# Turning u of two MLPs: from TensorE transposes to transposing DMAs on 16-bit halves

## The chip, the cores and the metric

The kernel runs on one core of one Trainium2 chip. A core has five engines that run their own instruction streams side by side: TensorE (PE in the profile, with its weight loads as PEld), VectorE (DVE), ScalarE (ACT), GpSimd (POOL) and SyncE (SP). All transfers of this kernel are issued from SP's queue, in order, and sixteen DMA engines carry them out. The metric is the device time of one execution in microseconds. The kernel before takes 2280.91 us in the median of three runs (2279.25 to 2284.33).

## The reference

The reference is a decoder trunk of two layers on 256 tokens of width 2048, in float32. Layer 0 has a convolution module as its token mixer, layer 1 differential attention, and each layer ends with the same kind of MLP. Every sub-layer scales and shifts its input by values made from a condition vector c (`mod = silu(c) @ ada_w + ada_b`), and ends in a LayerNorm. The part that the change touches is the MLP, which is computed twice:

```
def squared_relu_mlp(h, w1, b1, w2, b2):
    u = jnp.square(jax.nn.relu(h @ w1 + b1))
    return u @ w2 + b2
```

Here h is 256 x 2048, w1 is 2048 x 8192 and w2 is 8192 x 2048.

## The kernel before

**Arithmetic.** Each float32 operand of a large product is split into a high part (rounded to the float32r type) and a low part (the rest). A product is made of three matmuls: high by high, high by low, low by high (L700, L702, L703). The weights are split on the way: a 1 MB tile of 128 x 2048 comes from memory into one of four `raw` buffers, and each of its two halves is cast by ACT into `wh` (L655, "cast" below) and subtracted by DVE into `wl` (L657). There are four buffers each for `wh` and `wl` (`N_SP = 4`), so the cast of a half can run when PE has left the half four places before it.

**Tiling of an MLP.** The 8192 hidden columns are worked off in four quarters (q = 0 to 3). A quarter has four groups of w1 (g = 0 to 3), each making 512 columns of u for both token tiles (t = 0, 1), and then four groups of w2, which add that quarter's share of the output. A group has 4 weight tiles, so 8 halves, and a half feeds 12 matmuls of 128 x 512. In the two MLPs together there are 32 groups of w1, 16 each.

**Turning u.** A group of w1 leaves `h @ w1` in PSUM with tokens on the partitions, and w2 needs it with hidden columns on the partitions. `on_t1` is called when a token tile of a group is complete: ACT copies the PSUM tile to SBUF (`us`, L1452); two ticks later (`U_WAIT = 2`, a tick is one half) PE turns it by four 128 x 128 transposes into another PSUM tile (`ut`, L1458). Bias, relu and square follow: in the first MLP relu with bias on ACT in four pieces (L1464) and the square on ACT for q = 0 (L1467) and on DVE for the rest (L1469); in the second MLP an addition (L1471) and a max-multiply (L1474) on DVE. At last ACT casts the result to `u_hi` (L513) and DVE subtracts to `u_lo` (L516). All this is `on_t1` with its inner `rest`, and `put_split`. u's parts are read by w2's matmuls; the four groups of u are used one after the other, 4 of 16 chunks each.

**What else runs then.** During the first MLP, and the first quarter of the second, rows of `ada_w` come in as 1 MB tiles (`adaw`) through the same four `raw` buffers, and DVE takes their dot product with the condition (L228, one instruction of 2048 columns per tile). Small transfers bring rows for the residual (`basem_gb`, `basem_b`).

**What sets the order.** The kernel is written as a list of jobs whose steps are recorded in program order, with `defer(n, f)` putting a step n ticks later. A scheduler of the framework then sorts every engine's instructions by its own estimate of time. On the chip each engine works off its stream strictly in that order: an instruction whose operand is late holds all that stand behind it on its engine. The same holds for SP: a transfer that waits for a buffer or a source holds the transfers behind it.

Of the kernel before, what the change touches and what calls it, by code (L numbers as in the profile page):

```python
# [11 lines left out]
F32 = mybir.dt.float32  # L12
F32R = mybir.dt.float32r
I32 = mybir.dt.int32
AF = mybir.ActivationFunctionType
ALU = mybir.AluOpType
AX = mybir.AxisListType
# [2 lines left out]
P = 128  # L20
# [5 lines left out]
NG = 512  # L26
# [21 lines left out]
AHEAD = 4  # L48
POOL_LO = ()
U_WAIT = 2  # L50
POOL_LEAD = ()
POOL_TAIL = ()
GF_LOAD = 16
# [102 lines left out]
def trunk(  # L156
# [8 lines left out]
    nc = tc.nc  # L165
# [5 lines left out]
    work = ctx.enter_context(tc.tile_pool(name="work", bufs=2))  # L171
# [69 lines left out]
    def defer(n, fn):  # L241
        put_off.append((ticks[0] + n, fn))
# [265 lines left out]
    def put_split(pair, c0, n, s0, ns, src, eng=None, trail=False):  # L508

        hi, lo = pair  # L510
        h = hi[:, c0:c0 + n, s0:s0 + ns]
        l = lo[:, c0:c0 + n, s0:s0 + ns]
        nc.scalar.copy(h, src)  # L513

        def low():
            (eng or nc.vector).tensor_tensor(l, src, h.bitcast(F32), op=ALU.subtract)  # L516
        if trail:
            trailing.append(low)
        else:
            low()  # L520
# [464 lines left out]
    for g in range(NGRP):  # L985
# [3 lines left out]
    cv = {}  # L989

    cv.update(pw1b=vec1[:, 96:128], dwb=vec1[:, 128:144], clng=vec1[:, 144:160], clnb=vec1[:, 160:176],
              b1c=vec1[:, 176:304], lnc=vec1[:, 304:432], subg=vec1[:, 432:434])
# [267 lines left out]
    for s, (f0, nf) in enumerate(SLICES):  # L1260
# [6 lines left out]
        for pos, k in units:  # L1267
            g = group_order(s)[pos]
# [136 lines left out]
    for q in range(4):  # L1405
        defer(4 + q, lambda q=q: alpha_x(q))

    def mlp(i, ln_g, ln_b, gcol, bcol, pump, at_end, start=None, mid=None, last=None):
        gate, sc, cur = {}, {}, {}
        st = stats_tile(f"mlp{i}")  # L1410
# [35 lines left out]
        for q in range(4):  # L1446
            for g in range(4):
                n0 = q * D + g * NG

                def on_t1(t, ps, q=q, g=g, n0=n0):  # L1450
                    us = work.tile([P, NG], F32, tag="A", name=f"us_{i}_{q}_{g}_{t}")
                    nc.scalar.copy(us, ps)  # L1452
                    uT = cur["uT"]

                    def rest():
                        pt = tp_tile(f"ut_{i}_{q}_{g}_{t}")
                        for j in range(4):
                            nc.tensor.transpose(out=pt[:, j * P:(j + 1) * P], in_=us[:, j * P:(j + 1) * P],  # L1458
                                                identity=ident)
                        r = work.tile([P, 4, P], F32, tag="B", name=f"r_{i}_{q}_{g}_{t}")  # L1460
                        f0 = i * 64 + n0 // P
                        if i == 0:
                            for j in range(4):
                                nc.scalar.activation(r[:, j, :], pt[:, j * P:(j + 1) * P], AF.Relu,  # L1464
                                                     bias=cv["b1c"][:, f0 + j:f0 + j + 1])
                            if q == 0:
                                nc.scalar.activation(r, r, AF.Square)  # L1467
                            else:
                                nc.vector.tensor_tensor(r, r, r, op=ALU.mult)  # L1469
                        else:  # L1470
                            nc.vector.tensor_tensor(r, pt.rearrange("p (a n) -> p a n", a=4),  # L1471
                                                    cv["b1c"][:, f0:f0 + 4].unsqueeze(2).broadcast_to([P, 4, P]),
                                                    op=ALU.add)
                            nc.vector.scalar_tensor_tensor(r, r, 0.0, r, ALU.max, ALU.mult)  # L1474
                        put_split(uT, g * 4, 4, t * P, P, r, trail=True)
                    defer(U_WAIT, rest)
                first = q == 0 and g == 0
                add_group(f"w1_{i}_{q}_{g}", lambda: cur["hT"], wtiles(mlp_w1[i], 0, KC, n0), pump=pump, lead=(i + 1) * first,
                          start=(lambda q=q: begin_q(q)) if g == 0 else None,
                          pre_t=pre_t if first else None, on_t=on_t1, prep=(i == 1, prep) if first else None,  # L1480
                          between=ada_between if first and i == 0 else None)
            for n in range(4):
                def on_t2(t, ps, q=q, n=n):
                    add_gated(ps, gate["gb"], t, n, f"w2g_{i}_{q}_{n}_{t}")
                    if q == 3:
                        nc.vector.bn_stats(st[t][:, n, :], z[:, t, n * NG:(n + 1) * NG])
                        if n == 3:
                            return at_end(st, t)
                        if last is not None and t == 1 and n in (1, 2):
                            last["product"](t, n)  # L1490
                add_group(f"w2_{i}_{q}_{n}", lambda: cur["uT"], wtiles(mlp_w2[i], q * KC, KC, n * NG), pump=pump,
                          start=(lambda q=q: begin_w2(q)) if n == 0 else None,
                          tail=(q == 3 and n == 3) * (2 if last is None else 3), on_t=on_t2)
# [385 lines left out]
```

## Time and profile before

| | |
|---|---|
| median of 3 runs | 2280.91 us (2279.25 to 2284.33) |
| the profiled execution's own time | 2280.64 us |
| its span, first to last instruction | 2278.9 us |
| busy in the span | PE 2244.4 us, DVE 1714.8 us, ACT 1082.1 us, POOL 38.3 us |
| granted TensorE clock | 0.996 |
| moved by DMA | 608.58 MB, 267 GB/s in the mean |
| first MLP, about | 416 to 1146 us of the span |
| second MLP, about | 1546 to 2240 us of the span |

Times in the profile are counted from the first instruction. A row of the groups' view gives line, engine, operation, output and inputs, shape, how often, then busy microseconds, the mean nanoseconds of one, and the engine's idle time just before such instructions with what ended it. A row of the timeline starts with start and duration in microseconds. The windows' view gives for each stretch the busy time of each engine and how many instructions, then the granted clock, the mean busy share of the sixteen DMA engines and the rate.

### The profile page before, as it was taken

Reading aid. Unit: us, or ns where it says so; the run is one execution under the profiler, and the core shown is the slowest. Engines: PE = TensorE matmul, PEld = TensorE weight load, DVE = VectorE, ACT = ScalarE, POOL = GpSimd, SP = SyncE. Lnnn points to the kernel's source line nnn. Section 1 sums busy time; section 2 is a strip of 40 time slices with the busy share of each in tenths; the row PEclk is TensorE's granted clock in tenths of the full one; section 3 lists DMA queues with packets and bytes.
Section 4 is the critical chain, followed back from the end, with each engine's and each line's share of the span. In section 5 each row is a group of like instructions: output and inputs, shape, how many; then the busy total and the mean of one; then the engine's idle time right before and its main releaser. Section 6 shows DMA issues by size and latency. Waiting matters only on the chain.

```text
span 2278.9 us, 28170 instructions
## 1 busy us (share of the span) xinstructions
PE 2244.4 (98%) x11060; PEld 1797.1 (79%) x11060; DVE 1714.8 (75%) x2124; ACT 1082.1 (47%) x1488; POOL 38.3 (2%) x53
## 2 busy tenths in 40 slices
PE   8999999999999999999999999999999999999999
PEld 5677657687888888888878888877888888888886
DVE  7687989787978888777878877877866565655656
ACT  4336763564355355355454445545444444443442
POOL 0000000000000000000000010100000000000000
PEclk9999999999999999999999999999999999999999
DMA  9996789699988988988757766775965555556563
GB/s 397 420 394 257 312 324 396 215 338 323 347 302 305 320 288 309 325 290 311 279 176 248 241 222 208 279 269 172 331 233 188 186 194 193 185 185 203 185 222 111
DMA packets 217473, 608.58 MB, mean 267 GB/s; under 512 B 10382, under 2 KB 10610, under 8 KB 187770
## 3 DMA queue, kind: packets, MB, share of 16 engines
q1 hardware_dynamic: 217340, 606.78, 74.6%
q8 instruction: 87, 1.43, 0.3%
q14 instruction: 46, 0.38, 0.0%
HBM read 604.59 MB, written 2.15 MB: 266 GB/s over the span
## 4 chain that ended last, share of the span: by engine, by line
PE 87%; DVE 6%; ACT 3%; DMA 3%; issue 1%; POOL 0%; SPq 0%; ACTq 0%; DVEq 0%; POOLq 0%
PE w_ps L700 20%; PE w_ps L702 20%; PE w_ps L703 20%; PE pw_ps L598 2%; PE pw_ps L599 2%; PE pw_ps L600 2%; PE cv L934 1%; PE pw_ps L700 1%; PE pw_ps L703 1%; PE ut L1458 1%; PE qkv_v_ps L703 1%; PE pw_ps L702 1%; PE qkv_v_ps L700 1%; PE qkv_v_ps L702 1%; PE qkv_q_ps L703 1%; PE qkv_q_ps L700 1%
## 5 line engine op out<-in xcount | busy, mean ns | idle before, releaser
L655 ACT CAST wh_w<-w_w 128x1024 fp32r<-128x1024 f32 x512 | 536.2, 1054 | 692.1 <-PE w_ps L703 524.4
L657 DVE TENSOR_TENSOR wl_w<-w_w,wh_w 128x1024 fp32r<-128x1024 f32 x510 | 614.4, 1221 | 330.5 <-ACT wh_w L655 330.3
L700 PE MATMUL w_ps<-wh_w,hm_hi 128*128 128x512 f32 x1024 | 402.3, 393 | 2.4 <-ACT hm_hi L513 2.4
L702 PE MATMUL w_ps<-wl_w,u_hi 128*128 128x512 f32 x1024 | 399.1, 390 | 2.3 <-DVE wl_w L657 2.3
L703 PE MATMUL w_ps<-wh_w,hm_lo 128*128 128x512 f32 x1024 | 399.5, 390 | 1.6 <-DVE hm_lo L516 1.6
L700 PE MATMUL w_ps<-wh_w,u_hi 128*128 128x512 f32 x1024 | 399.5, 390 | 0.0
L702 PE MATMUL w_ps<-wl_w,hm_hi 128*128 128x512 f32 x1024 | 399.5, 390 | 0.0
L703 PE MATMUL w_ps<-wh_w,u_lo 128*128 128x512 f32 x1024 | 398.6, 389 | 0.0
L228 DVE SCALAR_TENSOR_TENSOR adaw<-adaw,cond_rows 128x2048 f32<-128x2048 f32 x108 | 246.6, 2284 | 0.1
L700 PEld LDWEIGHTS w_ps<-wh_w,hm_hi 128*128 128x128 f32 x1024 | 192.7, 188 | 44.6 <-ACT hm_hi L513 3.9
L703 PEld LDWEIGHTS w_ps<-wh_w,hm_lo 128*128 128x128 f32 x1024 | 192.7, 188 | 43.2 <-DVE hm_lo L516 2.9
L702 PEld LDWEIGHTS w_ps<-wl_w,u_hi 128*128 128x128 f32 x1024 | 192.2, 188 | 43.6 <-DVE wl_w L657 4.4
L700 PEld LDWEIGHTS w_ps<-wh_w,u_hi 128*128 128x128 f32 x1024 | 192.2, 188 | 40.3
L703 PEld LDWEIGHTS w_ps<-wh_w,u_lo 128*128 128x128 f32 x1024 | 192.2, 188 | 40.1
L702 PEld LDWEIGHTS w_ps<-wl_w,hm_hi 128*128 128x128 f32 x1024 | 192.8, 188 | 39.0
L598 PE MATMUL pw_ps<-wh_pw,h_hi 128*128 128x512 f32 x256 | 103.8, 405 | 2.2 <-ACT wh_pw L580 1.5
L599 PE MATMUL pw_ps<-wl_pw,h_hi 128*128 128x512 f32 x256 | 100.8, 394 | 0.9 <-DVE wl_pw L583 0.8
L600 PE MATMUL pw_ps<-wh_pw,h_lo 128*128 128x512 f32 x256 | 100.6, 393 | 0.0
L583 DVE TENSOR_TENSOR wl_pw<-w_pw,wh_pw 128x1024 fp32r<-128x1024 f32 x64 | 77.2, 1219 | 28.9 <-ACT wh_pw L580 28.6
L580 ACT CAST wh_pw<-w_pw 128x1024 fp32r<-128x1024 f32 x64 | 65.9, 1051 | 44.6 <-PE pw_ps L600 27.9
L598 PEld LDWEIGHTS pw_ps<-wh_pw,h_hi 128*128 128x128 f32 x256 | 48.4, 189 | 29.3 <-issue 12.6
L516 DVE TENSOR_TENSOR u_lo<-r,u_hi 128x512 fp32r<-128x512 f32 x64 | 43.5, 688 | 19.1 <-ACT u_hi L513 17.9
(350 smaller groups left out, 2991.2 us busy)
## 6 DMA issues: line engine op xcount, KB each, us to landing
w_w<-in_mlp_w_dram SPq DMA_DIRECT2D x256, 1024.0 KB, 5.5
adaw<-in_ada_rows_dram SPq DMA_DIRECT2D x108, 1024.0 KB, 6.9
w_pw<-in_pw_tiles_dram SPq DMA_DIRECT2D x32, 1024.0 KB, 11.6
ad<-in_ada_rows_dram SPq DMA_DIRECT2D x25, 1024.0 KB, 8.8
w_pw<-in_conv_pw_w_dram SPq DMA_DIRECT2D x16, 1024.0 KB, 9.7
w_qkv_q<-in_attn_qkv_w_dram SPq DMA_DIRECT2D x16, 1024.0 KB, 5.1
w_qkv_k<-in_attn_qkv_w_dram SPq DMA_DIRECT2D x16, 1024.0 KB, 5.0
w_qkv_v<-in_attn_qkv_w_dram SPq DMA_DIRECT2D x16, 1024.0 KB, 6.7
```

The costliest lines, as they stand in the source:

```text
L228: nc.vector.scalar_tensor_tensor(w, w, 1.0, cond_rows, ALU.mult, ALU.mult, accum_out=m[:, ch:ch + 1])
L516: (eng or nc.vector).tensor_tensor(l, src, h.bitcast(F32), op=ALU.subtract)
L580: nc.scalar.copy(hq, rq)
L583: nc.vector.tensor_tensor(lq, rq, hq.bitcast(F32), op=ALU.subtract)
L598: nc.tensor.matmul(pss[t], lhsT=xh, rhs=wh, start=(kc == first), stop=False)
L599: nc.tensor.matmul(pss[t], lhsT=xh, rhs=wl, start=False, stop=False)
L600: nc.tensor.matmul(pss[t], lhsT=xl, rhs=wh, start=False, stop=(kc == last))
L655: nc.scalar.copy(hi, rq)
L657: eng.tensor_tensor(lo, rq, hi.bitcast(F32), op=ALU.subtract)
L700: nc.tensor.matmul(pss[tt], lhsT=xh, rhs=wh, start=(kc == 0 and job["bias"] is None), stop=False)
L702: nc.tensor.matmul(pss[tt], lhsT=xh, rhs=wl, start=False, stop=False)
L703: nc.tensor.matmul(pss[tt], lhsT=xl, rhs=wh, start=False, stop=(kc == nk - 1))
```

## The change

In both MLPs (`BY_DMA = (0, 1)`) u is now turned by DMA in place of PE. The DMA turns 16-bit elements, so each float32 is handled as two of them. `on_t1` hands over to a new function `halves_t`, which, for each token tile of a group, does the following:

- ACT copies the PSUM tile to SBUF as before (now L1419), save for g = 1, t = 1 (`DIRECT`), where this copy is left out and the next step reads PSUM.
- ACT copies the tile once more (L1421), as 1024 elements of 16 bits, so that the 512 first halves stand together and then the 512 second halves.
- SP issues a transposing DMA within SBUF (L1423), 128 x 1024 elements of 16 bits in eight blocks of 128 x 128.
- Four ticks later in the program (`T_WAIT = 4`), ACT joins the halves again into float32 (L1427), and bias, relu, square and split follow, from SBUF and not from PSUM. In the first MLP's q = 0 the square moves from ACT to DVE.

There are 64 token tiles in the two MLPs, 8 of them direct.

```diff
+T_WAIT = 4
+BY_DMA = (0, 1)
+DIRECT = ((1, 1),)
...
+    def halves_t(t, ps, uT, i, q, g, n0):
+
+        name = f"{i}_{q}_{g}_{t}"
+        room = work.tile([P, 2, NG], F32, tag="X", name=f"us_{name}", bufs=3)
+        us = ps
+        if (g, t) not in DIRECT:
+            us = room[:, 0, :]
+            nc.scalar.copy(us, ps)
+        parts = room[:, 1, :].bitcast(U16).rearrange("p (b n) -> p b n", b=2)
+        nc.scalar.copy(parts, us.bitcast(U16).rearrange("p (n b) -> p b n", b=2))
+        turned = work.tile([P, 2, 4, P], U16, tag="A", name=f"ux_{name}")
+        nc.sync.dma_start_transpose(turned.rearrange("p b a n -> p (b a) n"), parts.rearrange("p b n -> p (b n)"))
+
+        def rest():
+            r = work.tile([P, 4, P], F32, tag="B", name=f"r_{name}")
+            nc.scalar.copy(r.rearrange("p a n -> p (a n)").bitcast(U16).rearrange("p (a n b) -> p a n b", a=4, b=2),
+                           turned.rearrange("p b a n -> p a n b"))
+            f0 = i * 64 + n0 // P
+            if i == 0:
+                for j in range(4):
+                    nc.scalar.activation(r[:, j, :], r[:, j, :], AF.Relu, bias=cv["b1c"][:, f0 + j:f0 + j + 1])
+                nc.vector.tensor_tensor(r, r, r, op=ALU.mult)
+            else:
+                nc.vector.tensor_tensor(r, r, cv["b1c"][:, f0:f0 + 4].unsqueeze(2).broadcast_to([P, 4, P]), op=ALU.add)
+                nc.vector.scalar_tensor_tensor(r, r, 0.0, r, ALU.max, ALU.mult)
+            put_split(uT, g * 4, 4, t * P, P, r, trail=True)
+        defer(T_WAIT, rest)
...
                 def on_t1(t, ps, q=q, g=g, n0=n0):
+                    uT = cur["uT"]
+                    if i in BY_DMA:
+                        return halves_t(t, ps, uT, i, q, g, n0)
                     us = work.tile([P, NG], F32, tag="A", name=f"us_{i}_{q}_{g}_{t}")
                     nc.scalar.copy(us, ps)
-                    uT = cur["uT"]
```

**The order on ACT.** The example is the first MLP, q = 1, g = 1. Names end in a number of the tile: `wh_w1_0_1_2_3_0` is the high part of w1 in MLP 0, quarter 1, group 2, tile 3, half 0; `us_0_1_1_0` is MLP 0, quarter 1, group 1, token tile 0. Before, ACT has from the end of the group on:

```order
L1452 COPY us_0_1_1_0_5560<-w1_0_1_1_ps0_5387 128x512
L1452 COPY us_0_1_1_1_5562<-w1_0_1_1_ps1_5388 128x512
L655 CAST wh_w1_0_1_2_1_1_5566<-w_w1_0_1_2_1_5542 128x1024
L655 CAST wh_w1_0_1_2_2_0_5610<-w_w1_0_1_2_2_5608 128x1024
L1464 ACTIVATE r_0_1_1_0_5587<-ut_0_1_1_0_5582,vec1_101 128x128 x4
L1464 ACTIVATE r_0_1_1_1_5599<-ut_0_1_1_1_5594,vec1_101 128x128 x4
L513 CAST u0_1_hi_5237<-r_0_1_1_0_5587 128x4x128
L655 CAST wh_w1_0_1_2_2_1_5626<-w_w1_0_1_2_2_5608 128x1024
L513 CAST u0_1_hi_5237<-r_0_1_1_1_5599 128x4x128
L655 CAST wh_w1_0_1_2_3_0_5648<-w_w1_0_1_2_3_5646 128x1024
```

Now, from the copy of the 16-bit halves on:

```order
L1421 COPY us_0_1_1_0_5549<-us_0_1_1_0_5549 128x1024
L1421 COPY us_0_1_1_1_5554<-w1_0_1_1_ps1_5385 128x1024
L659 CAST wh_w1_0_1_2_1_1_5560<-w_w1_0_1_2_1_5531 128x1024
L659 CAST wh_w1_0_1_2_2_0_5578<-w_w1_0_1_2_2_5576 128x1024
L659 CAST wh_w1_0_1_2_2_1_5594<-w_w1_0_1_2_2_5576 128x1024
L1427 COPY r_0_1_1_0_5614<-ux_0_1_1_0_5552 128x1024
L1427 COPY r_0_1_1_1_5622<-ux_0_1_1_1_5556 128x1024
L1432 ACTIVATE r_0_1_1_0_5614<-r_0_1_1_0_5614,vec1_101 128x128 x4
L1432 ACTIVATE r_0_1_1_1_5622<-r_0_1_1_1_5622,vec1_101 128x128 x4
L659 CAST wh_w1_0_1_2_3_0_5634<-w_w1_0_1_2_3_5632 128x1024
L659 CAST wh_w1_0_1_2_3_1_5650<-w_w1_0_1_2_3_5632 128x1024
L517 CAST u0_1_hi_5228<-r_0_1_1_0_5614 128x4x128
```

Three casts of weights now stand between the halves and the first join, the two joins and the relus stand ahead of the casts of tile 3, and the casts to `u_hi` behind these.

**The order on DVE.** At the same place DVE has before:

```order
L657 TENSOR_TENSOR wl_w1_0_1_2_1_1_5567<-w_w1_0_1_2_1_5542,wh_w1_0_1_2_1_1_5566 128x1024
L1469 TENSOR_TENSOR r_0_1_1_0_5587<-r_0_1_1_0_5587 128x512
L1469 TENSOR_TENSOR r_0_1_1_1_5599<-r_0_1_1_1_5599 128x512
L516 TENSOR_TENSOR u0_1_lo_5238<-r_0_1_1_0_5587,u0_1_hi_5237 128x4x128
L516 TENSOR_TENSOR u0_1_lo_5238<-r_0_1_1_1_5599,u0_1_hi_5237 128x4x128
L657 TENSOR_TENSOR wl_w1_0_1_2_2_0_5611<-w_w1_0_1_2_2_5608,wh_w1_0_1_2_2_0_5610 128x1024
```

and now:

```order
L661 TENSOR_TENSOR wl_w1_0_1_2_2_1_5595<-w_w1_0_1_2_2_5576,wh_w1_0_1_2_2_1_5594 128x1024
L232 SCALAR_TENSOR_TENSOR adaw_1_1_15_5598,mod_1_1_4612<-adaw_1_1_15_5598,cond_rows_108 128x2048
L235 TENSOR_TENSOR mod_1_1_4612<-mod_1_1_4612,vec1_101 128x16
L1433 TENSOR_TENSOR r_0_1_1_0_5614<-r_0_1_1_0_5614 128x512
L1433 TENSOR_TENSOR r_0_1_1_1_5622<-r_0_1_1_1_5622 128x512
L520 TENSOR_TENSOR u0_1_lo_5229<-r_0_1_1_0_5614,u0_1_hi_5228 128x4x128
L520 TENSOR_TENSOR u0_1_lo_5229<-r_0_1_1_1_5622,u0_1_hi_5228 128x4x128
L661 TENSOR_TENSOR wl_w1_0_1_2_3_0_5635<-w_w1_0_1_2_3_5632,wh_w1_0_1_2_3_0_5634 128x1024
```

The u steps of the group stood ahead of the low part of tile 2, half 0; they now stand ahead of that of tile 3, half 0, and so they do in all 32 groups.

**The order on SP.** Again the same group; the transposing DMAs stand between the loads:

```order
L640 DMA w_w1_0_1_2_2_5576<-in_mlp_w1_dram 128x4x512
L423 DMA adaw_1_1_15_5598<-in_ada_rows_dram 128x2048
L1423 DMA_TRANSPOSE ux_0_1_1_0_5552<-us_0_1_1_0_5549 128x8x128
L1423 DMA_TRANSPOSE ux_0_1_1_1_5556<-us_0_1_1_1_5554 128x8x128
L640 DMA w_w1_0_1_2_3_5632<-in_mlp_w1_dram 128x4x512
```

Before, the load of tile 3 followed the `adaw` load directly. It now stands behind both transposes, and each of these waits on SP until ACT has written its halves. Where no `adaw` comes in (the second MLP from q = 1 on), the loads run further ahead, and the load behind the transposes is that of tile 1 of the group after the one that PE has just begun.

More of the change, by code (lines that the diff above doesn't have):

```diff
@@ L14 @@
 I32 = mybir.dt.int32
+U16 = mybir.dt.uint16
 AF = mybir.ActivationFunctionType
```

## The prediction

> **What bounds the kernel now.** I read the page first, then the windows by stage, then the chain of waits.
>
> ```profile
> span 2278.9 us, 28170 instructions
> PE 2244.4 (98%) x11060; PEld 1797.1 (79%) x11060; DVE 1714.8 (75%) x2124; ACT 1082.1 (47%) x1488; POOL 38.3 (2%) x53
> PE 87%; DVE 6%; ACT 3%; DMA 3%; issue 1%; POOL 0%; SPq 0%; ACTq 0%; DVEq 0%; POOLq 0%
> ```
>
> TensorE is busy for 98% of the span, and 87% of the chain that ended last is PE. A busy share over all stages can hide a stage with another limit, so the windows of the stages that the change touches come next (columns: stretch, length, PE, PEld, DVE, ACT, POOL, granted clock, DMA share, GB/s).
>
> ```profile
> 500.00:600.00 100.00, 97.68 (x434) 79.17 (x434) 83.42 (x88) 44.45 (x64) 0.00 (x0) 1.00 0.92 329
> 735.00:912.00 177.00, 177.00 (x798) 146.65 (x797) 147.31 (x178) 84.52 (x119) 0.00 (x0) 1.00 0.86 306
> 1760.00:1937.00 177.00, 177.00 (x796) 146.76 (x795) 103.19 (x104) 75.59 (x81) 0.00 (x0) 1.00 0.59 190
> ```
>
> In a quarter of the first MLP (735 to 912) PE has no gap, but DVE is at 83% and the DMA engines at 86%. In a quarter of the second (1760 to 1937) PE has no gap either, with DVE at 58% and DMA at 59%. So PE bounds both, and work taken off PE shortens them as long as nothing else gets late. The first MLP has little room for that, the second a lot.
>
> **What is removed.** The 256 transposes. Their own durations (272 ns each) overlap, so the price on PE is read from the chain, which holds what they hold up; and the step of the matmuls from PE's timeline.
>
> ```profile
> 1781.95 0.87 PE ut L1458 x8
> L1458 PE MATMUL ut<-ident,us x256: 270/272/273, 455.9 to 2183.2; 128*128 128x128 f32 x128
> 1737.33 0.39 PE L700 MATMUL w_ps<-wh_w,hm_hi 128*128 128x512 f32 x1
> 1738.01 0.39 PE L700 MATMUL w_ps<-wh_w,hm_hi 128*128 128x512 f32 x1
> ```
>
> Eight transposes, both token tiles of a group, take 0.87 us. 32 groups make 27.9 us: the gain if nothing is late. Three matmuls take 0.68 us, one 0.227, a half of 12 matmuls 2.72 and a group of 8 halves 21.8. These give the clock for the rest.
>
> **What is added on ACT and DVE.**
>
> ```profile
> L655 ACT CAST wh_w<-w_w 128x1024 fp32r<-128x1024 f32 x512 | 536.2, 1054 | 692.1 <-PE w_ps L703 524.4
> L657 DVE TENSOR_TENSOR wl_w<-w_w,wh_w 128x1024 fp32r<-128x1024 f32 x510 | 614.4, 1221 | 330.5 <-ACT wh_w L655 330.3
> L1452 ACT COPY us<-w_ps 128x512 f32<-128x512 f32 x64 | 37.4, 587 | 32.6 <-PE w_ps L703 30.0
> L516 DVE TENSOR_TENSOR u_lo<-r,u_hi 128x512 fp32r<-128x512 f32 x64 | 43.5, 688 | 19.1 <-ACT u_hi L513 17.9
> L513 ACT CAST u_hi<-r 128x512 fp32r<-128x512 f32 x64 | 39.8, 635 | 21.5 <-DVE r L1474 20.1 <-DVE r L1469 1.4
> 839.19 2.17 ACT L1464 ACTIVATE r<-ut,vec 128x128 f32<-128x128 f32 x8
> ```
>
> Separating and joining write 1024 elements a partition each, as L655 does: 1.05 us is their price, bounded below by 0.59 (L1452, the same bytes as 512 elements) and above by twice 1.05, since no row has 16-bit elements. 128 of them less 8 copies spared are 130 us on ACT. In a group of the first MLP ACT then has 8 casts (8.4), copies (1.2), halves and joins (4.2), relus (2.2) and `u_hi` (1.3): 17.3 of 21.8 us. Busy time is no limit. DVE gets 8 squares, 5.5 us in all, in q = 0 of the first MLP, where its idle time hides them; without that cover they would cost these 5.5.
>
> **What is added as waits.** This decides. In the new order DVE does the low part of tile 3, half 0 of the next group (call it W) only behind `u_lo`, and so behind the joins. Count from e, the start of the `us` copy. PE leaves the group at e + 0.7 and reaches tile 3 after six halves, at e + 17.0; the second matmul there needs W, at e + 17.2. In the first MLP, from the start J of the second join, W is done at J + 1.05 (join) + 2.2 (relus) + 2.1 (two casts) + 1.25 (two `u_hi`) + 0.7 (`u_lo`) + 1.2 (W) = J + 8.5. So J may be e + 8.7. The cast ahead of the joins can run when PE leaves a half:
>
> ```profile
> 1778.58 1.27 ACT L1452 COPY us<-w_ps 128x512 f32<-128x512 f32 x2 [0.98 <-PE w_ps L703]
> 1781.98 1.05 ACT L655 CAST wh_w<-w_w 128x1024 fp32r<-128x1024 f32 x1 [1.19 <-PE w_ps L703]
> ```
>
> Here e is 1778.58 and tile 2, half 0 was cast at e + 3.4, as counted; half 1 is due 2.72 later at e + 6.1 and ends at e + 7.2, so the joins start at 7.2 and J is e + 8.2 at best: 0.5 us to spare. The first transpose is issued at e + 1.7 (copy and halves), the second at about e + 4.3 (both tiles' copies and halves and a cast), so the second must land within 4.4 us.
>
> ```profile
> 834.56 0.34 SPq L419 DMA_DIRECT2D adaw<-in_ada_rows_dram  x1
> 834.84 1.27 ACT L1452 COPY us<-w_ps 128x512 f32<-128x512 f32 x2 [0.27 <-PE w_ps L703]
> 836.77 0.37 SPq L636 DMA_DIRECT2D w_w<-in_mlp_w_dram  x1
> w_w<-in_mlp_w_dram SPq DMA_DIRECT2D x71, 1024.0 KB, 7.1
> adaw<-in_ada_rows_dram SPq DMA_DIRECT2D x41, 1024.0 KB, 7.3
> DMA to landing us min/median/max: 5.0/5.2/5.4
> out_dram<-z SPq DMA_DIRECT2D x8, 256.0 KB, 2.0
> DMA packets 217473, 608.58 MB, mean 267 GB/s; under 512 B 10382, under 2 KB 10610, under 8 KB 187770
> q1 hardware_dynamic: 217340, 606.78, 74.6%
> GB/s 397 420 394 257 312 324 396 215 338 323 347 302 305 320 288 309 325 290 311 279 176 248 241 222 208 279 269 172 331 233 188 186 194 193 185 185 203 185 222 111
> ```
>
> In the example of the first MLP an `adaw` load leaves 0.3 us before e, and such loads land after 7.3 us in the median there (7.1 for weights), against 5.2 in 1760 to 1937. No row shows a transposing DMA. Its price X on the rings has these bounds. Below: 256 KB land in 2.0 us and 1024 KB in 5.2, so 256 KB more cost 1.07 us; X is 1.0 if turning is free. Above: 217340 packets took 74.6% of 16 engines' 2278.9 us, 0.125 us each; were each row of 128 elements a packet (1024 of them), X would be 1024 x 0.125 / 16 = 8.0. I take 1.3, near the lower end, because 256-byte rows are no larger in sum and only their number speaks for more; both ends stay for the range.
>
> The Trainium skill ("DMA: Bandwidth & Descriptors", section "Latency and other measured facts") gives 261 GB/s for a transposing DMA with a non-contiguous middle dimension. X would be 1.0 by it and the sum 2257; no run here shows it.
>
> With the queue free of older bytes at about e + 6, and one microsecond from the last byte to the signal, the second transpose lands at e + 7 + 2X: 9.6 for X = 1.3, so about 0.9 late for an order like the example. Not every group has that order. Where the two `u_hi` stand ahead of the casts of tile 3, about 3 us more are free and nothing is late. In four groups the second `u_hi` stands behind one more cast, which PE frees at e + 14.3: W then ends at 14.3 + 1.05 + 0.6 + 0.7 + 1.2 = e + 17.9, 0.7 late whatever X is. I take 0.5 us a group in the mean at X = 1.3, 0.2 at 1.0, and 2 us more per us of X beyond 1.3, as two transposes go first. The load of tile 3 behind them agrees: it moves from e + 1.9 (836.77) to e + 4.4, gets the rings at e + 6 + 2X, needs 2.6 us at the 400 GB/s of the page's first slices and one to land, e + 12.2, from where W is done 5.3 later (two casts, two `u_hi`, `u_lo`, W): e + 17.5, 0.3 late.
>
> This holds for the 20 groups that have `adaw` loads beside them (16, and q = 0 of the second MLP). In the other 12 the example's J is met with 3 to 5 us to spare: there are no relus on ACT, the rings are 41% free, and the load behind the transposes is wanted only some 15 us later. They cost nothing up to X of about 3; without that cover, the same 2 us per us of X.
>
> Sum: 2280.64 (profiled; 0.27 under the median) - 27.9 + 20 x 0.5 = 2262.7. **I predict 2263 us.**
>
> **Rivals.**
>
> Full gain, 2253 us: X is 1.0 or less, and the landings find gaps in the rings. For it: the 24% between 306 GB/s and those 400. Against it: the 7 us that loads take there.
>
> No change, 2281: X is from 1.6 to 1.9, and 20 groups at 1.1 to 1.7 us (1.4 at X = 1.75) give the gain back. For it: the 0.5 us to spare for J. Against it: so narrow a band of X.
>
> Slower: the transposes are slow on the rings. At X = 2.5 the 20 groups wait 0.5 + 2.4 = 2.9 us each, 58 us: 2311. At X = 4 it is 5.9, 118 us, and some 2 in the other 12: about 2395. It decides from X = 1.75 on, at the place where DVE holds W behind `u_lo`. For it: packets at 0.125 us. Against it: the slope of 1.07 us, at which plain rows go.
>
> Slower by ACT: the join reads two bytes in turn from places 1 KB apart, and costs 2.1 instead of 1.05. Both joins of a group stand ahead of W, so the 20 groups wait 2.1 more, 42 us: 2305. Against it: ACT's casts at L580 read their tile in a changed order, in long runs, and take the 1051 ns of a plain one.
>
> ```profile
> L580 ACT CAST wh_pw<-w_pw 128x1024 fp32r<-128x1024 f32 x64 | 65.9, 1051 | 44.6 <-PE pw_ps L600 27.9
> ```
>
> For this last rival speaks the Trainium skill ("SBUF — State Buffer", section "Specifications (TRN2)"): 16-byte lines need two or more hits each for the full rate. L580's row does not test that; no run here does.
>
> **How the numbers follow.** Forecast (X from 1.0 to 1.6): 0.42. Full gain: 0.17. No change: 0.11. Slow transposes: 0.22. Slow joins: 0.08. A measurement of this kernel tells some 0.2%, 4.6 us, from no change. Faster is the first two cases, 0.59; the same 0.11; slower 0.30. The forecast's own range is 2256 to 2275. The 8-in-10 range reaches down to 2248, the full gain and some gaps of PE in the first MLP (2.3 us in 500 to 600) closed, and up to 2308, which leaves out the slow transposes from X of 2.4.
>
> **What would show it.** The transposes' landing in the DMA view: under 6 us beside the second MLP's quarters and 5 to 7 beside the first's. The copies at L1421 and L1427 at 1.05 us. PE gap-free in the second MLP from q = 1 on, where a quarter takes 177 - 3.5 = 173.5 us; in the first MLP, gaps of half a microsecond ahead of L702, ended by DVE's `wl_w`, with ACT's L1427 waiting for DMA before them. I am wrong if L1427 waits several microseconds for each transpose, if the second MLP shows gaps too, or if L1427 takes 2 us.

## The result and the profile after

The changed kernel takes 2308.15 us in the median of four runs (2305.62 to 2309.88), beside 2281.3 for the kernel before on the same chip. The ratio is 1.011, with a 95% interval of 1.0097 to 1.0123: it is slower by 1.1%, where the prediction had 2263 and faster. The page of the changed kernel answers to the lines of the page before:

```profile
span 2307.8 us, 27925 instructions
PE 2233.3 (97%) x10804; PEld 1777.3 (77%) x10804; DVE 1718.0 (74%) x2132; ACT 1203.0 (52%) x1600; POOL 38.3 (2%) x53
q1 hardware_dynamic: 284924, 623.56, 78.8%
PE 70%; DVE 10%; DMA 10%; ACT 7%; issue 3%; POOL 0%; SPq 0%; ACTq 0%; DVEq 0%; POOLq 0%
```

PE is busy 11 us less than before, not 28, and its share of the chain fell from 87% to 70%, to the good of DMA, DVE and ACT. The windows (columns as in the prediction) show where:

```profile
500.00:600.00 100.00, 94.75 (x406) 76.31 (x405) 85.45 (x93) 52.05 (x68) 0.00 (x0) 0.98 0.98 343
600.00:735.00 135.00, 128.43 (x554) 104.89 (x553) 100.50 (x100) 80.57 (x109) 0.00 (x0) 0.98 0.95 309
735.00:912.00 177.00, 173.29 (x756) 141.84 (x756) 141.39 (x172) 95.03 (x121) 0.00 (x0) 0.99 0.94 308
1790.00:1963.00 173.00, 173.00 (x765) 143.31 (x764) 102.43 (x104) 91.33 (x95) 0.00 (x0) 1.00 0.67 206
```

The quarter of the second MLP (the last row, its q = 1) has no gap. The first MLP, gap-free before from 735 to 912, has gaps, and its granted clock is under 1.00. The waits of PE, ACT and DVE (us in total, times, the longest) name the chain:

```profile
PE w_ps L706 <- DVE wl_w L661: 31.8, 20, 3.4
ACT r L1427 <- DMA ux<-us: 30.7, 26, 3.6
DVE r L1433 <- ACT r L1432: 40.6, 21, 5.0
DVE u_lo L520 <- ACT u_hi L517: 24.4, 20, 3.7
```

Apart from the transposes, both kernels give PE the same 10804 matmuls in the same order. So the start of each can be set against the start of the same one before. The growth of the difference, stage by stage, from the two traces (gap: PE's idle times over 50 ns; half clock: time at a granted clock of 0.5; before in brackets; us):

```
stage                             difference   gap          half clock
up to the first MLP                  -1.5      13.2 (12.3)   6.8 (10.2)
first MLP, q = 0                     +8.1      10.7 (3.1)    6.8 (0)
           q = 1                     +7.4       6.6 (0)      6.8 (0)
           q = 2                     +7.6       8.2 (0)      3.4 (0)
           q = 3                     +5.8       6.8 (0)      3.4 (0)
attention, with its joints           +8.1      16.7 (11.2)  10.2 (6.8)
second MLP, q = 0                    +4.3       4.3 (0)      6.8 (0)
            q = 1, 2, 3              -3.6 each  0.7 (0.7)    0 (0)
sum                                 +29.0
```

So the gain is there, 0.89 us a group, wherever nothing gets late: in the last 12 groups. The 20 groups with `adaw` loads beside them lose 33.2 us net, and the attention, of which no instruction was moved, 8.1.

One stall from start to end, the first MLP's q = 3, g = 2, where e, the start of the `us` copy, is 1057.15. First the rows of SP and ACT that matter from the timeline, others left out between them, then the chain of waits (start, us, what):

```profile
1053.38 0.34 SPq L423 DMA_DIRECT2D adaw<-in_ada_rows_dram  x1
1055.56 0.37 SPq L640 DMA_DIRECT2D w_w<-in_mlp_w_dram  x1
1057.15 0.59 ACT L1419 COPY us<-w_ps 128x512 f32<-128x512 f32 x1 [0.98 <-PE w_ps L707]
1057.83 0.34 SPq L423 DMA_DIRECT2D adaw<-in_ada_rows_dram  x1
1058.84 5.88 SPq L1423 DMA_TRANSPOSE ux<-us  x2
1064.82 1.87 SPq L640 DMA_DIRECT2D w_w<-in_mlp_w_dram  x2
1067.88 2.25 ACT L1427 COPY r<-ux 128x1024 uint16<-128x1024 uint16 x2 [3.55 <-DMA ux<-us]
```

```profile
1058.84 9.01 DMA ux<-us
1067.88 2.25 ACT r L1427 x2
1070.12 1.37 ACT r L1432 x5
...
1072.48 1.74 ACT wh_w L659 x2
...
1074.27 0.62 ACT u_hi L517
...
1074.91 0.56 DVE u_lo L520
...
1076.12 1.23 DVE wl_w L661
```

Three loads of 1 MB leave in the 5.5 us ahead of the first transpose, which lands 9 us after its issue. ACT stands at the join for 3.55 us. From there joins, relus, casts, `u_hi`, `u_lo` and the low part follow as the prediction counted them, and the low part is done at 1077.35, e + 20.2, where PE wanted it at e + 17.2. PE's gap is 3.06 us. What a gap does beyond its length stands in PE's timeline of another one, in q = 1, g = 3:

```profile
729.19 0.39 PE L704 MATMUL w_ps<-wh_w,u_hi 128*128 128x512 f32 x1
732.60 0.50 PE L706 MATMUL w_ps<-wl_w,u_hi 128*128 128x512 f32 x1 [3.02 <-DVE wl_w L661]
...
734.28 0.63 PE L706 MATMUL w_ps<-wl_w,u_hi 128*128 128x512 f32 x1
734.71 0.63 PE L707 MATMUL w_ps<-wh_w,u_lo 128*128 128x512 f32 x1
...
737.26 0.40 PE L707 MATMUL w_ps<-wh_w,u_lo 128*128 128x512 f32 x1
```

After 3.02 us of waiting, the matmuls between 733.9 and 737.3 start 0.43 us apart where the step is else 0.227. The last section comes back to that.

### The profile page after: what moved, and what is told of

The parts are those of the page before. It is cut to its first block, busy times and chain, and to the rows that moved or that the text cites. A ratio compares the mean times of both kernels' runs of the same rounds, so it can differ in the third digit from the quotient of the medians.

```text
span 2307.8 us, 27925 instructions
## 1 busy us (share of the span) xinstructions
PE 2233.3 (97%) x10804; PEld 1777.3 (77%) x10804; DVE 1718.0 (74%) x2132; ACT 1203.0 (52%) x1600; POOL 38.3 (2%) x53
## 3 DMA queue, kind: packets, MB, share of 16 engines
q1 hardware_dynamic: 284924, 623.56, 78.8%
## 4 chain that ended last, share of the span: by engine, by line
PE 70%; DVE 10%; DMA 10%; ACT 7%; issue 3%; POOL 0%; SPq 0%; ACTq 0%; DVEq 0%; POOLq 0%
PE w_ps L706 16%; PE w_ps L707 15%; PE w_ps L704 15%; DMA w_w<-in_mlp_w_dram 3%; DMA ux<-us 3%; DVE wl_w L661 2%; PE pw_ps L602 2%; ACT wh_w L659 2%; PE pw_ps L604 2%; PE pw_ps L603 2%; PE cv L938 1%; PE pw_ps L704 1%; PE pw_ps L707 1%; PE pw_ps L706 1%; PE qkv_q_ps L704 1%
## 5 line engine op out<-in xcount | busy, mean ns | idle before, releaser
L706 PE MATMUL w_ps<-wl_w,hm_hi 128*128 128x512 f32 x1024 | 404.8, 395 | 21.2 <-DVE wl_w L661 21.2
L706 PE MATMUL w_ps<-wl_w,u_hi 128*128 128x512 f32 x1024 | 400.6, 391 | 10.6 <-DVE wl_w L661 10.6
L232 DVE SCALAR_TENSOR_TENSOR adaw<-adaw,cond_rows 128x2048 f32<-128x2048 f32 x108 | 246.8, 2285 | 1.4 <-DMA adaw<-in_ada_rows_dram 1.4
L706 PEld LDWEIGHTS w_ps<-wl_w,hm_hi 128*128 128x128 f32 x1024 | 194.9, 190 | 67.7 <-DVE wl_w L661 27.5
L706 PEld LDWEIGHTS w_ps<-wl_w,u_hi 128*128 128x128 f32 x1024 | 193.0, 189 | 53.2 <-DVE wl_w L661 13.4
L1427 ACT COPY r<-ux 128x1024 uint16<-128x1024 uint16 x64 | 74.1, 1172 | 30.8 <-DMA ux<-us 30.7
## 6 DMA issues: line engine op xcount, KB each, us to landing
w_pw<-in_conv_pw_w_dram SPq DMA_DIRECT2D x16, 1024.0 KB, 10.2
```

Source lines behind the costliest of these rows:

```text
L232: nc.vector.scalar_tensor_tensor(w, w, 1.0, cond_rows, ALU.mult, ALU.mult, accum_out=m[:, ch:ch + 1])
L706: nc.tensor.matmul(pss[tt], lhsT=xh, rhs=wl, start=False, stop=False)
L1427: nc.scalar.copy(r.rearrange("p a n -> p (a n)").bitcast(U16).rearrange("p (a n b) -> p a n b", a=4, b=2), turned.rearrange("p b a n -> p ...
```

## Experiments

Each was timed beside the kernel before on the same chip. The theory at the start: the stalls are made inside the first MLP, where DVE's low part of tile 3 stands behind `u_lo`, and so behind joins that wait for a landing.

**Where the loss is.** e1, only the second MLP by DMA:

```diff
-BY_DMA = (0, 1)
+BY_DMA = (1,)
```

> Only the second MLP turns u by DMA (BY_DMA = (1,)); the first is as before. Matched matmul by matmul, the changed kernel loses 29 us against the one before in the first MLP, 1.5 behind it, 6.5 in the attention, 4.3 in the first quarter of the second MLP, and gains 10.6 in the other three quarters. Theory (the first MLP's loss is made in it, by transposes and weight loads that land late; the attention's is not the change's, no instruction of it moved): 2281 + 4.3 - 10.6 = 2275, the attention as before. Rival (the attention's 6.5 us belong to the change, for instance through buffers): 2281 or more.

Measured: 2278.09, ratio 0.9979 (0.9969 to 0.9989). Matched as above, the first MLP is as before to within 0.6 us, the attention +0.4, the second MLP's q = 0 +4.3 and the rest -10.4. The median misses the theory's 2275 by 3, the profiled execution, at 2275.76, by less than 1; the attention's loss did not come along.

e2, only the last 12 groups:

```diff
-                    if i in BY_DMA:
+                    if i == 1 and q > 0:
```

> Only the 12 groups of the second MLP from its second quarter on turn u by DMA, those that have no loads of ada rows beside them. Theory: they gain 0.88 us each without a stall, 10.6 us: 2281 - 10.6 = 2270, ratio 0.9953. Rival (the attention's loss comes with the change): 2277. That DVE or ACT get late there without the quarters before: over 2275, with gaps of PE ended by wl_w behind 1790 us.

Measured: 2269.06, ratio 0.994 (0.9925 to 0.9954), three quarters at -3.6 us each, all else within 0.5 of before from the first MLP on. Where the rings have room, the change does what it says.

**Which load makes it.** e3, ACT's work without a transfer:

```diff
-        turned = work.tile([P, 2, 4, P], U16, tag="A", name=f"ux_{name}")
-        nc.sync.dma_start_transpose(...)
+        turned = parts.rearrange("p b (a n) -> p b a n", a=4)
```

> The transposing DMA is left out and the joins read ACT's separated halves, so u isn't turned; all of ACT's copies and joins stay, and DVE's low part of tile 3 stays behind u_lo. Theory (what is late is the transfers: the transposes' landing and the loads behind them on SP and on the rings): the stalls of the first MLP go, 2281 - 28 = 2253, up to 2262 with a few small gaps. Rival (ACT's own 4 us more per group, ahead of the casts, make the low parts late whatever the DMA does): the first MLP keeps gaps of PE of 1 us and more a group, 2280 to 2300.

Measured: 2268.96, ratio 0.9941 (0.9923 to 0.9959), between the two. The first MLP's quarters: +5.8, -3.6, -2.6, -0.5. ACT's extra work (and DVE's squares) does cost about 9 us in q = 0, next to nothing in q = 1 and 2, and 3 in q = 3. The scheduler, with no landing to expect, also put the joins earlier on ACT, mostly by one or two casts.

e6, the transfers without ACT's work:

```diff
-                    if i in BY_DMA:
-                        return halves_t(t, ps, uT, i, q, g, n0)
...
                     nc.scalar.copy(us, ps)
+                    ux = work.tile([P, 8, P], U16, tag="X", name=f"ux_{i}_{q}_{g}_{t}", bufs=3)
+                    nc.sync.dma_start_transpose(ux, us.bitcast(U16))
```

> The kernel before, PE turning u as before, and beside it the 64 transposing DMAs, issued from us behind its copy into a tile that nobody reads: no halves, no joins, nobody waits for a landing. Theory (the weight loads get late by the engines' time of the transposes and by SP holding): the first MLP stalls by itself, 15 to 30 us: 2296 to 2311, its quarters losing 4 us or more each, the second MLP's last three nothing. Rival (the loss is ACT's waiting for the landing, ahead of the casts): 2281 to 2286.

Measured: 2295.43, ratio 1.0062 (1.0047 to 1.0077). The total is near the theory's lower end, but not its places: +10.3 in the first MLP's q = 0, +2.3 in the second's, and 0.0 in the first MLP's q = 1, 2 and 3. There the transfers alone hold up nothing, which is the rival's case.

e9, both loads, but no join waits:

```diff
-                           turned.rearrange("p b a n -> p a n b"))
+                           parts.rearrange("p b (a n) -> p a n b", a=4))
```

> The transposing DMAs are issued as in the changed kernel, but nobody reads what they write: the joins take the halves from ACT, so u isn't turned. Both loads are there, the transfers' and ACT's, without the wait that ties them. Alone, the transfers cost the first MLP 10 us, all in its first quarter, and ACT's work 9 there and 4 in the other three; the changed kernel loses 8 in the first and some 11 in each of the others, before the gain of 3.5. Theory (in quarters 1 to 3 the loss is ACT's standing still at a join until the transposes land, with the casts behind it): quarters 1 to 3 stay within 2 us of the gain of 3.5 each, 2276 to 2290 in all. Rival (late loads and a later ACT together are enough): quarters 1 to 3 lose 5 to 8 us each as in the changed kernel, 2298 to 2308.

Measured: 2281.17, ratio 0.9995 (0.9986 to 1.0005). The quarters q = 1 to 3: -3.4, -1.2, -1.1, as the theory said, against +7.4, +7.6, +5.8 in the changed kernel. The wait is not the only difference: as in e3 the joins stand earlier on ACT, mostly by one or two casts, and SP has a load between the two transposes in 9 of the first MLP's 16 groups, where the changed kernel has one in 3. So this run fits the wait as the cause and does not show it by itself; the 21 groups below do that by the order. In q = 0 it is +7.6: there the two loads need no wait to do harm.

**The turning, or the wait.** e5, a plain transfer of the same size:

```diff
-        nc.sync.dma_start_transpose(turned.rearrange("p b a n -> p (b a) n"), parts.rearrange("p b n -> p (b n)"))
+        nc.sync.dma_start(turned.rearrange("p b a n -> p (b a n)"), parts.rearrange("p b n -> p (b n)"))
```

> The transposing DMA is replaced by a plain one of the same 256 KB between the same tiles, so u isn't turned. With no transfer at all the time was 2269, with the transposing ones 2308: the transfers are worth 39 us. Theory (the price is that of turning: some 1056 packets under 512 bytes, 1.85 us of all sixteen engines and 1.27 us of SP for each): a plain one costs 0.6 to 1.1 us of the engines and 0.35 of SP, and at least half of the 39 come back: 2270 to 2288. Rival (it is the waiting: SP holds the weight loads behind a transfer that waits for ACT, whatever the transfer is, and the joins wait for a landing): most of the 39 stay, 2295 to 2308.

Measured: 2301.53, ratio 1.0089 (1.0074 to 1.0104). The rival's number came: 6.6 us of the 39 are back. The row of the queue on this kernel's page (packets, MB, share of sixteen engines):

```profile
q1 hardware_dynamic: 226556, 623.56, 75.9%
```

The transfer's own rows, of this kernel and then of the changed one (duration on SP min/median/max in ns, landing in us):

```profile
L1423 SPq DMA_DIRECT2D ux<-us x64: 464/471/738, 454.2 to 2206.7; - x64
DMA to landing us min/median/max: 2.2/4.5/8.6
```

```profile
L1423 SPq DMA_TRANSPOSE ux<-us x64: 1233/1273/5116, 452.8 to 2213.1; - x64
DMA to landing us min/median/max: 3.0/4.1/8.7
```

From q1's share, 75.9% of 2301.3 against 74.6% of 2278.9 us, a plain one takes 46.6 / 64 = 0.73 us of all sixteen engines; the transposing one takes (78.8% of 2307.8 - 1700.1) / 64 = 1.85. The landing rows rest on the 31 of the 64 transfers for which the trace gives a landing. In the first MLP, behind loads, these land after 5.9 us in the median, the transposing ones after 5.3 (17 each); in the last 12 groups, where the rings have room, after 2.3 and 3.1 (10 each). And the second join of a group starts at e + 11.0 in the mean of the first MLP's 16 groups, against e + 10.8. Behind 1 MB loads the cheaper transfer brought the joins nothing.

e7, issued from ACT, out of SP's queue:

```diff
-        nc.sync.dma_start_transpose(
+        nc.scalar.dma_start_transpose(
```

> The transposing DMAs are issued by ACT and not by SP; the weight loads no longer stand behind them. ACT has the issue in its own stream, directly behind the halves, and pays for it some 1.2 us each, if it takes there what it took on SP. Theory that SP's holding makes the loads late: 2270 to 2290. Rival (the engines' time and the joins' wait decide, not SP): 2300 to 2325, since ACT gets 2.5 us more per group on top.

Measured: 2455.64, ratio 1.0779 (1.0725 to 1.0833), far beyond both. The rows of the transposes, with ACT's idle time ahead of the joins (us, times):

```profile
L1423 ACTq DMA_TRANSPOSE ux<-us x64: 1247/1306/11216, 454.6 to 2350.4; - x64
...
  DMA ux<-us: 155.0, 49
...
DMA to landing us min/median/max: 3.0/6.6/28.2
```

The loads no longer stood behind the transposes, and the joins waited five times as long (155.0 us for 30.7). So taking the transposes off SP did not help. A clean test of SP's holding this is not: ACT's own stream was held by the issues, up to 11.2 us, and the landings (given for 30 of the 64) got later, so the 147 us more have several causes that this run does not separate.

**A smaller set.** e8, the 17 groups that showed no stall:

```diff
-                    if i in BY_DMA:
+                    if (q > 0 and g == 0) if i == 0 else (q > 0 or g > 1):
```

> u is turned by DMA in the 17 groups that showed no stall in the changed kernel: the second MLP's last 12, the last two of its first quarter, and the first group of the first MLP's quarters 1 to 3; PE turns the other 15. Theory (a group that finds the engines free costs nothing, and stalls don't come from groups before it): 2281 - 17 x 0.88 = 2266. Rival (groups beside ada loads were free only by the stalls ahead of them, in which loads caught up): as with 12 groups, 2270, or some us more.

Measured: 2278.01, ratio 0.9981 (0.9969 to 0.9993). The rival has the right sign, and it is worse than 12 groups: in the first MLP q = 1 and 2 lose 1.7 and 3.7, the second's q = 0 2.5. This fits the rival's reason, that a group which looked free was so by the stall ahead of it, in which the loads caught up; nothing here shows that step by itself.

**The order.** e4, in all 32 groups, DVE's low parts ahead of `u_lo`:

```diff
-T_WAIT = 4
+T_WAIT = 6
```

> T_WAIT = 6 for 4: in the order, DVE's low parts of tile 3 now stand ahead of the squares and u_lo in nearly all groups; ACT's joins and the transposes stay where they were but for a place or two. Theory (the price is paid where the low part of tile 3 stands behind u_lo, which waits for the joins): that low part then needs J + 5.5 and not J + 8.5 us, J being the start of the second join, 3 us more to spare per group, more than most stalls measured (1.3 to 3.4 us): 2258 to 2272. Rival (the weight loads of tile 3 themselves are late, held on SP behind the transposes and then slow on full rings, so that the casts are late whatever DVE's order is): at least half the stalls stay, 2285 to 2305.

Measured: 2304.61, ratio 1.0091 (1.0074 to 1.0107), the rival's number, but not for its reason. A new wait appears among PE's:

```profile
PE w_ps L706 <- DVE wl_w L661: 17.7, 15, 2.5
PE w_ps L704 <- ACT u_hi L517: 16.3, 5, 7.2
```

The wait for the low parts fell from 31.8 to 17.7, and PE now waits for `u_hi`: the last group of a quarter (g = 3) hands its u to w2 too late. So the groups g = 0, 1, 2 have to be looked at apart from g = 3, as the table below does.

e10, the joins behind ACT's casts of tile 3 as well:

```diff
-T_WAIT = 4
+T_WAIT = 6
...
+            with tc.issue_after(raws["cast"].ins):
-            nc.scalar.copy(r..., turned...)
+                nc.scalar.copy(r..., turned...)
...
-            nc.scalar.copy(hi, rq)
+            raws["cast"] = nc.scalar.copy(hi, rq)
```

> As the changed kernel, but with both joins bound behind ACT's casts of the next group's tile 3 (T_WAIT = 6 and an explicit dependence), so a late landing holds no cast up to the half H + 7; the squares and u_lo stand behind the low parts of tile 3 on DVE. The joins then start at e + 12.6, by when the transposes have landed in nearly all groups, and the low part of half H + 8 is done at e + 22.4 with 22.7 as its limit, by the durations of the profile. Theory (the wait for the landing, in front of casts, is the price): the stalls of quarters 1 to 3 of the first MLP fall from 7 us each to under 2.5, the total to 2266 to 2288. Rival (the loads are late by the queue alone): 2298 to 2308.

Measured: 2313.3, ratio 1.0142 (1.0126 to 1.0157); above both ranges. Again g = 3 pays (19.6 us in q = 1 to 3), which neither side had counted, and the first MLP's q = 0 loses 12.2.

e11, now with g = 3 and the first MLP's q = 0 left to PE, and the second MLP's q = 0 too; `u_lo` of the nine groups left in the first MLP goes another two ticks later:

```diff
-                    if i in BY_DMA:
+                    if q > 0 and (i == 1 or g < 3):
...
-            put_split(uT, g * 4, 4, t * P, P, r, trail=True)
-        defer(T_WAIT, rest)
+            hi, lo = [x[:, g * 4:g * 4 + 4, t * P:(t + 1) * P] for x in uT]
+            nc.scalar.copy(hi, r)
+            def low():
+                nc.vector.tensor_tensor(lo, r, hi.bitcast(F32), op=ALU.subtract)
+            if i == 0:
+                defer(2, low)
+            else:
+                trailing.append(low)
+        defer(T_WAIT + 2 * (i == 0), rest)
```

beside the explicit dependence of the edit before.

> DMA turns u in 21 groups: the last 12 of the second MLP as the changed kernel orders them, and the first three groups of the first MLP's quarters 1 to 3, with the joins behind the casts of tile 3 and u_lo another two halves later, so that the low part of half H + 8 has 2.6 us to spare. Theory (with the wait moved off the casts these nine groups gain their 0.88 us too): 2281 - 12 - 8 = 2261, ratio 0.991. Rival (room on the engines is what the first MLP lacks): no better than with 12 groups, 2269 or more.

Measured: **2262.9** (2259.76 to 2264.07), ratio 0.9917 (0.99 to 0.9933): the best version, 0.8% faster than the kernel before. In its windows PE has no gap, though the rings are as full as in the changed kernel (0.98 and 0.93):

```profile
630.00:735.00 105.00, 105.00 (x469) 87.03 (x468) 84.52 (x84) 67.23 (x97) 0.00 (x0) 1.00 0.98 331
735.00:912.00 177.00, 177.00 (x787) 146.37 (x786) 149.94 (x181) 98.21 (x131) 0.00 (x0) 1.00 0.93 320
```

Was it the order, or only that g = 3 and q = 0 were left out? e12, the same 21 groups in the changed kernel's order (only the condition of the last edit):

> The same 21 groups as the kernel at 2263, but all in the changed kernel's own order: T_WAIT = 4, joins ahead of the casts of tile 3, the low parts of tile 3 behind u_lo. In the changed kernel the first three groups of the first MLP's quarters 1 to 3 lose 9.4 us in sum, at 2263 they gain 8.0. Theory (the order is the price: the low part of tile 3 behind u_lo, behind joins that wait for a landing): the nine lose again, 2272 to 2282. Rival (their loss was a backlog made by the first quarter's groups and the last ones of each quarter, which PE turns here): 2260 to 2265.

Measured: 2279.25, ratio 0.9987 (0.9972 to 1.0001), in the theory's range: it is the order.

e13, the same 21, with `T_WAIT + 2 * (i == 0)` alone. In the traces this puts DVE's low parts of tile 3 ahead of the squares and `u_lo`, while ACT's joins stay ahead of its casts of tile 3; ACT's `u_hi` goes back by one to four casts:

> Again the 21 groups; in the nine of the first MLP T_WAIT is 6, so that the low parts of tile 3 stand ahead of u_lo, but the joins stay ahead of ACT's casts of tile 3. With T_WAIT = 6 in all 32 groups, the first three groups of quarters 1 to 3 together gained 2.0 us and the last ones lost 19.7, their gaps ended by u_hi: u came too late for w2. Theory (moving the low parts ahead of u_lo was right, and hidden by that new wait): 2260 to 2267. Rival (the joins on ACT, ahead of casts, are the price, wherever DVE has u_lo): 2270 to 2280.

Measured: 2271.03, ratio 0.9955 (0.9935 to 0.9975), in the rival's range, with part of the theory's gain. The growth of the difference over the nine groups (first MLP, q = 1 to 3, g = 0 to 2) and over the three with g = 3, in us, from the matched matmuls; a group without a stall shows -0.89:

```
                                              nine groups   g = 3
changed kernel (all 32)                          +9.4       +11.4
e4, two ticks later (all 32)                     -0.8       +22.2
e10, joins behind casts too (all 32)             +2.9       +19.6
e9, joins wait for nothing (all 32)              -3.4        -2.3
e12, 21 groups, old order                        +8.5         0
e13, 21 groups, low parts first                  -2.2         1.5
e11, 21, joins behind casts, u_lo later          -8.1         0.5
```

With the same groups and as many transfers, the order with DVE's low parts ahead of `u_lo` is 10.7 us better, and the one with the joins behind the casts and `u_lo` further back another 5.9. This is from one trace of each; by the medians, each less that of the kernel before beside it, the two steps are 8.2 and 7.2 us. In each step more than one thing moved (`u_hi` in the first, joins and `u_lo` in the second), and these are not told apart.

Are late weight loads the price, as the rivals of e4 and e10 have it? The waits of ACT's casts for them, in the kernel before, the changed one and e11:

```profile
ACT wh_w L655 <- DMA w_w<-in_mlp_w_dram: 127.6, 49, 7.1
ACT wh_w L659 <- DMA w_w<-in_mlp_w_dram: 96.4, 38, 6.7
ACT wh_w L659 <- DMA w_w<-in_mlp_w_dram: 157.7, 60, 6.9
```

They are longest in e11, the fastest of the three. What e11 lacks is the joins' wait for a landing: 1.2 us in all, against 30.7 in the changed kernel.

## Why the prediction was wrong

**What is removed** was right: 0.89 us a group where nothing is late, against 0.87.

**ACT's prices** were right within 12%: L1421 takes 1046 ns in the median and L1427 1172 (1.05 taken for both). The rival of slow joins (2.1) did not come. That DVE's squares in q = 0 of the first MLP hide in idle time did not hold as told: without any transfer that quarter lost 9 us. How much of it is the squares and how much ACT's is not separated.

**The place** was right: the low part of tile 3 on DVE, behind `u_lo`, behind the joins; the 21 groups in three orders show it, and the signs named for it came: gaps ahead of L706, ended by `wl_w`, with L1427 waiting for DMA before them. The last 12 groups were right too, at -10.8 for -10.5 us, with landings of 3.1 to 4.1 us in the ten transfers for which the trace gives one, as was said for under 6.

**The step that failed** is the landing, "With the queue free of older bytes at about e + 6 ... the second transpose lands at e + 7 + 2X", which made the time J of the second join hang on the transfer's price X. It gave J = e + 9.6, 0.9 us late; measured is e + 10.8 in the mean of the first MLP's 16 groups (8.3 to 14.1). The DMA packets of the traces, put to their issues by number and size, show the parts:

```
first MLP, mean of 16 groups, us from e     changed kernel   e5, plain
bytes of the older loads done                     6.6           6.7
first join starts                                 8.4           8.5
second join starts (J)                           10.8          11.0
X                                                 1.85          0.73
(older bytes done) + 1 + 2X                      11.3           9.2
```

The free queue was nearly right in the mean (3.4 to 9.1 from group to group; 7.4 in the example above, where three loads took 3.4 us each and not the 2.6 counted). What was wrong is what follows it. In the mean the first join starts 1.8 us behind the older bytes, whichever transfer it waits for. The second starts 2.4 or 2.5 us behind the first: at least the join itself, and more where ACT has a cast or relus between the two, or where SP issues a load of 1 MB between the two transfers (3 groups, with J at 12.3 to 14.1; in e5 5 groups, 10.1 to 15.6). With the X that was measured, 1.85 for 1.3, the formula comes near, but by luck: with 0.73 it gives 9.2, and 11.0 is measured. So in these two kernels J does not hang on X, and the break-even at X = 1.75, on which three cases and their chances were built, is not borne out. The microsecond from the last byte to the signal has no row behind it; in the changed kernel's loads it is 0.4 us in the median.

**From J to the low part** 8.5 us were counted; 7.0 to the end of `u_lo` and 1.2 for the low part are measured. With J at 10.8 the low part is 1.8 us late in the mean.

**The price of 0.5 us a group** was mis-sized as a consequence: the 20 groups lost 33.2 + 20 x 0.88 = 50.8 us, 2.5 each. By the prediction's own slope the measured X would give 1.6 each, and 2285 us. Their gaps are 33.5 us (36.6 less the 3.1 of before), and two terms were missing from the sum: PE at half clock for 27.3 us after gaps, which cost about 11.5 by the number of matmuls that ran in them, and some 0.16 us for each new start, since the step is 0.227 and a matmul on its own takes 0.39, about 3.6 in 22 stalls. Together these are 48.6 of the 50.8; the rest is not accounted for. It was probably also wrong to take each group by itself: a held cast holds a raw buffer, and so the load after next. e8's groups fit that.

**The attention** was not in the sum, and lost 8.1 us. No instruction of it was moved on any engine. In the other kernels it took from 0.3 us less than before to 5.9 more, with 0 to 10.2 us at half clock, and in e10, with as many transposes, 0.1 more. What sets it stays open.

**The range** reached to 2308, and the result lies just past it. The rival of slow transposes had its sign and its place, and 2311 at X = 2.5, but its cause, the transfer's price on the rings, is not the one that the runs show: e5, at 0.73 for 1.85, is only 6.6 us faster.

## What to carry to other kernels

Ask of a new transfer in the middle of a chain not what it costs but which loads are in the queue when it is issued, and put whatever waits for it behind the work on its engine that doesn't; in e11 rings at 0.98 did no harm once the casts and the low parts of tile 3 no longer stood behind the wait. A step that is moved back for this has its own deadline at its reader (here w2, for the last group of a quarter). And count a stall of PE that takes half of a 3.4 us window as costing up to 1.7 us more than its length.

## What was not expected

**The clock after a stall.** Around the gap shown above, in four windows of 3.4 us:

```profile
727.10:730.50 3.40, 2.48 (x11) 1.70 (x10) 1.16 (x2) 2.64 (x7) 0.00 (x0) 1.00 0.99 366
730.50:733.90 3.40, 1.30 (x6) 1.08 (x7) 3.32 (x5) 1.88 (x3) 0.00 (x0) 0.99 0.70 260
733.90:737.30 3.40, 3.40 (x10) 2.63 (x9) 3.40 (x4) 0.96 (x2) 0.00 (x0) 0.50 0.76 239
737.30:740.70 3.40, 3.40 (x16) 2.79 (x15) 3.37 (x5) 1.33 (x2) 0.00 (x0) 1.00 1.02 386
```

With PE busy 73% of a window the clock stays at 1.00; with 38% the next window is at 0.50. The periods at half clock in this trace last 3.41 us or twice that and lie on one grid, and each one, but for the last at the kernel's end, followed a period in which PE was busy 52% or less (one such period, at 51%, had no half clock behind it); the shortest gap that led to one by itself was 1.9 us. Inside the two MLPs there are 27.3 us of them (20.5 in the first, 6.8 in the second's first quarter), and none before the change. The Trainium skill ("TensorE: Matmul & The Clock Gate", section "Part 1: The HAM clock gate (the "warmup" mystery)") tells of a free-running window of 3413 ns and of half rate after an idle one; the trace agrees on length and rate, and shows that about half of it idle is enough.

**The transposing transfer.** 256 KB within SBUF are 1056 packets, against 144 for a plain one, take 1.85 us of all sixteen engines against 0.73, and hold SP for 1.27 us in the median, up to 5.1, against 0.47. The shortest landing is 3.0 us against 2.2. The Trainium skill ("Advanced Engine Details and Errata", section "X-Bar Transpose (TRN2)") has it that transposing DMAs are as fast as regular ones. By the engines' time the rows say two and a half times dearer here; by the landing behind other loads (5.3 and 5.9 us in the median of the first MLP) they agree, and with room on the rings they are 0.8 us apart (3.1 and 2.3).

**A second queue.** From ACT's queue, beside SP's with its loads of 1 MB, the same transposes landed up to 28.2 us after their issue, where behind those loads on one queue 8.7 was the longest of the landings that the traces give.
